# A decoder layer on one core: cached keys and values by pairs, other homes for values, low parts last

## The chip, the cores and the metric

The kernel runs on one core of a Trainium2 chip. The metric is device time in microseconds (us): the kernel before took 955.71 us, the median of three runs (954.79 to 956.05). The engines are named as in the profile: PE is TensorE with its matmuls, PEld its weight loads, DVE is VectorE, ACT is ScalarE, POOL is GpSimd, SP is SyncE, which here only issues DMAs. A name with a q (SPq, ACTq) is an engine's queue in the act of issuing.

## What is computed

One layer of a hybrid decoder for a prompt of 512 rows and for 8 samples of 4 rows each, with the same weights, all in float32. Cut to what matters:

```python
z = rms_norm(x, g_mix_pre) @ w_in                 # 1024 -> mLSTM heads and attention heads
h_ml = mlstm_chunkwise(q, k, v, i_pre, logf, ...) # 4 heads of 128
s = einsum('bqhcd,bkhcd->bhcqk', dq, dk) * 64**-0.5     # differential attention:
p = softmax(where(mask, s, -inf))                       # two components c per head
a = p[:, :, 0] - lam * p[:, :, 1]
h_da = rms_norm(einsum('bhqk,bkhd->bqhd', a, dv), g_da_head) * (1 - lam_init)
x = x + rms_norm(concat([h_ml, h_da]) @ w_out, g_mix_post)
x = x + rms_norm(mem_attend(rms_norm(x, g_mem_pre), mk, mv, w_mq, w_mo), g_mem_post)
f, conv_new = conv_ffn(rms_norm(x, g_ffn_pre), conv_buf, w_up, w_dw, b_dw, w_down)
x = x + rms_norm(f, g_ffn_post)
```

In the attention the samples also read 256 cached positions each, whose pages of 128 lie scattered (cache_dk and cache_dv through page_table). In the cross-attention (mem_attend, 4 heads of 256) the prompt reads 256 memory rows, whose keys and values are computed from mem_prompt (w_mk, w_mv), and each sample reads 256 cached ones (cache_mem_k, cache_mem_v). The cached keys and values, too, go through TensorE only once.

## The kernel before

**Precision.** The large products are made from pairs: an operand is split into a high part (fp32r, a cast on ACT, L146 or L221) and a low part (the rest, a subtraction on POOL or DVE, L147 or L223), and a product is hi·hi + hi·lo + lo·hi, three matmuls (L409 to L411, L467, L479). Rows are normalised, turned by four transposes into one PSUM tile (tp, L330), scaled with the gain on the way out (ht, L332) and split into tiles named hT, hqT or fT: such a tile of four feature groups is a "quad", and two quads hold the 1024 features. In the numbered names, fT00 and fT01 are the high parts of quad 0 and 1, fT10 and fT11 the low parts. The 544 rows are blocks 0 to 3 of 128 prompt rows and block 4 with the 32 sample rows.

**Buffers.** Weights are loaded by SP into the staging pool (tiles wst, six buffers, L231) and split into slots (wslot, pool wp, four buffers with the tag W). `W.nslots` says how many slots may be filled ahead, and `W.pump()` fills them. A second pool, sp, has eleven general buffers (tag S). Two PSUM pools hold five tiles (mm) and three (at).

**What sets the order.** The program is written as coroutines that are stepped against each other, and a scheduler then orders the instructions of every engine; each engine runs its list strictly in that order. `tc.issue_after(x)` holds what stands in its block until x, and `burst(x)` (L343) is the same with high priority, so that a run of matmuls stays together.

**The start.** The memory rows are normalised and turned into memT; the ht tiles behind them are kept, and four DMAs of ACT write them to DRAM (mem_d, L598), held until the second result of the memory keys (mkv, L544). That result is turned (mkt, L548) and copied by ACT (mkT, L550).

**Differential attention.** The prompt's softmax runs as a pipeline of 16 steps: scores (sda, L1229), exponents on ACT (pda, L1233), transposes (tpa, L1245), their copy by ACT (aT, L1247), values (oda, L1255). The samples' cached keys are gathered by SP (L1087), turned into kT tiles (wp buffers, L1209, L1210) and multiplied by the samples' queries, which fill 32 columns (ssc, L1215, four matmuls for each sample). Their values are gathered into staging buffers and summed into ops (L1297, eight matmuls for each sample); a last four (L1305) add the samples' own rows. Two weight slots are reserved in this stage (`W.nslots = 2`), for w_out, whose staging loads stand behind the value gathers on SP.

**Cross-attention.** The samples' memory values come in four tiles of the wp pool (samples 3 to 6) and, for the other samples, in two staging buffers each. They are used in the order 2, 1, 0, 7, 6, 5, 4, 3, and the load of sample 7 is issued last, behind the products of 2, 1 and 0 (pso, L1464), whose staging buffers it takes.

**The way into the FFN.** proj_add makes the projection w_mo by blocks 4, 0, 1, 2, 3, adds it to the residual (xb, L1152), and appends the block to a list of those still to be turned (norm_turn). Here the rows are turned unscaled; their factors (rsd, L1164) are spread over the partitions by a matmul each (rsb, L1584), copied (L1585) and multiplied onto the FFN's first product (L1611). The last two blocks are turned inside the FFN's first four column tiles (gemmB with half_first), which take rows 0 to 255 first (128x256) and rows 256 to 543 after (128x288).

Of the kernel before, what the change touches and what calls it, by code (L numbers as in the profile page):

```python
# [1 line left out]

# [5 lines left out]
F32 = mybir.dt.float32  # L8
# [69 lines left out]
def kernel(ctx: ExitStack, tc: tile.TileContext, I, O):  # L78
# [241 lines left out]

    turned = [None]

    def norm_turn(h, n, gname, xt, c0, pool=(True, False)):

        tmps = []
        for q in range(2):
            ps = at("tp")
            pv = v2(ps, P)[:, :, :n]
            for j in range(4):
                turned[0] = tr(pv[:, j, :], h[:, (4 * q + j) * P:(4 * q + j + 1) * P], ident[:n, :n])  # L330
            tmp = T2([P, 4, n], "ht")
            VTT(out=tmp, in0=pv, in1=gcol(gname, 4 * q, 4 * q + 4).unsqueeze(2).broadcast_to([P, 4, n]), op=MUL)  # L332
# [64 lines left out]
    def gemmA(xt, nk, blocks, evac, block_major=False, before=None, mid=None, halves=False, midk=4):  # L397
# [29 lines left out]
        else:  # L427
# [27 lines left out]
                yield 4 * 0.53  # L455
            yield 0

    def gemmB(xt, evacs, half_first=False):

        if half_first:  # L460
            slots = [W.get() for _ in evacs]
            for i, (c0, c1) in enumerate(HALF):
                for s, ev in zip(slots, evacs):
                    ps = mmp()[:, :c1 - c0]
                    for k in range(8):
                        for j, (l, x) in enumerate(((0, xt.hi), (0, xt.lo), (1, xt.hi))):
                            mm(ps, lhsT=s[:, l, k, :], rhs=x(k, c0, c1), start=(k == 0 and j == 0), stop=(k == 7 and j == 2))  # L467
# [69 lines left out]
    evm = []  # L537

    def mem_k():
        dst = O["p_mem_k"][0, 0].rearrange("t h d -> t (h d)")  # L540
        for i in range(2):
            def ev(b, ps):
                t = Z("mkv")
                evm.append(nc.scalar.mul(out=t, in_=ps, mul=mrs[:, b:b + 1]))  # L544
                nc.scalar.dma_start(out=dst[b * P:(b + 1) * P, 512 * i:512 * i + 512], in_=t)
                pt = at("mkt")
                for j in range(4):
                    tr(pt[:, j * P:(j + 1) * P], t[:, j * P:(j + 1) * P], ident)  # L548
                u = Z("mkT")
                nc.scalar.copy(out=u, in_=pt)  # L550
                nc.scalar.dma_start(out=mk_d[:, 4 * i:4 * i + 4, b * P:(b + 1) * P], in_=v2(u, P))
            yield from gemmA(memT, 8, [0, 1], ev)
# [35 lines left out]
    for i, _ in enumerate(mem_k()):  # L588
        if i in HSTEPS:
            j = HSTEPS.index(i)  # L590
            norm_T(xbs[HB[j]], rows(HB[j])[1], "g_mix_pre", hT, rows(HB[j])[0])
            if j + 2 < 5:
                h_in(HB[j + 2])

    with tc.issue_after(evm[1].ins):
        for b in range(2):
            for q, t in enumerate(kept[b]):
                nc.scalar.dma_start(out=mem_d[:, 4 * q:4 * q + 4, b * P:b * P + P], in_=t)  # L598


    masks = T2([P, MASK_W], "masks")
# [510 lines left out]
    def proj_add(xt, gname, src, gname2, dst, order=None, scale=None):  # L1112

        g = gbc(gname)
        y0, s0, xb, pend, ready, target = {}, {}, {}, [], [], []

        def ssq(b, y, nm):
            n = rows(b)[1]
# [20 lines left out]
        def ev1(b, ps):  # L1139
# [6 lines left out]
            VTT(out=z, in0=ps, in1=g[:n, 512:], op=MUL)  # L1146
            STT(out=ss, in0=s0[b], scalar=EPS, in1=ss, op0=ADD, op1=ADD)
            rs = rstd(ss, n, 1, None)
            x = xb[b]
            for i, z in enumerate((y0[b], z)):  # L1150
                c = slice(512 * i, 512 * i + 512)
# [13 lines left out]
            scale[1].append((rs[:n], c0, n))  # L1165

        def mid():
            if len(pend) > LP:
                norm_turn(*pend.pop(0))

        def second(xt2):
            target.append(xt2)
            run(gemmA(xt, 8, [4, 0, 1, 2, 3], ev1, block_major=True, before=before, mid=mid, midk=1 if scale else MIDK))
            while ready:
# [35 lines left out]
            (VCP if g else nc.scalar.copy)(out=kt[:, :, g * P:(g + 1) * P], in_=v2(ps, P))  # L1210

    def dk_scores(b):
        ps = mmp("ssc")[:, :260]
        for h in range(H):
            mm(ps[NS * h:NS * h + NS], lhsT=qz[:, h, b // 4].rearrange("p c r -> p (c r)"), rhs=kts[b][:, h, :],  # L1215
               start=True, stop=True)
        VTT(out=ps[:, 256:260], in0=ps[:, 256:260], in1=con("cm4"), op=ADD)
        sample_exp(sall, b, ps, nm, su)

    def da_soft(i):  # L1220
        b, h = i // H, i % H
# [65 lines left out]
    vts = {}  # L1287

    def dv_load(b):
        st = vts[b] = stage()  # L1290
        for g in range(2):
            gather("cache_dv", b, g, st[:, 512 * g:512 * g + 512])

    def dv_out(b):
        for g in range(2):
            for h in range(H):
                mm(ops[NS * h:NS * h + NS, :P], lhsT=az[g][:, h, b * NS:(b + 1) * NS],  # L1297
                   rhs=vts[b][:, g * 512 + h * P:g * 512 + (h + 1) * P], start=(b == 0 and g == 0), stop=False)
# [5 lines left out]
    for h in range(H):  # L1304
        mm(ops[NS * h:NS * h + NS, :P], lhsT=anew[:, h].rearrange("p b t -> p (b t)"), rhs=dvS[:, h * P:(h + 1) * P],  # L1305
           start=False, stop=True)
    oS = T2([P, P], "daoS")
    nc.scalar.copy(out=oS, in_=ops[:, :P])
    sq = T2([P, P], "dasq")
# [135 lines left out]

    def mv_load(b):

        if 2 < b < 7:
            t = wp.tile([P, 2, DM], F32, name="vt", tag="W")
            vts[b] = [t[:, 0], t[:, 1]]  # L1450
        else:
            vts[b] = [stage(), stage()]
        for c in range(2):
            dma(out=vts[b][c], in_=I["cache_mem_v"][0, b, c * P:(c + 1) * P].rearrange("t h d -> t (h d)"))
# [123 lines left out]
    rss = []  # L1578

    def spread(i):  # L1580
        while rss and (i or len(rss) > 2):
            rs, c0, n = rss.pop(0)
            ps = at("rsb")
            mm(ps[:, :n], lhsT=rs.broadcast_to([n, P]), rhs=ident[:n, :n], start=True, stop=True)  # L1584
            VCP(out=rsb[:, c0:c0 + n], in_=ps[:, :n])  # L1585
# [63 lines left out]
    def ups_of(gi):  # L1649
# [248 lines left out]
```

## Time and profile before

| | |
|---|---|
| Runs without the profiler, median of 3 | 955.71 us (954.79 to 956.05) |
| The profiled execution's own time | 956.55 us |
| Its span, first to last instruction | 954.8 us |
| Mean granted TensorE clock | 0.997 |
| Instructions | 17089 |
| DMA traffic | 130.27 MB, mean 136 GB/s |

The 40 slices of the span show how evenly TensorE is loaded. Each digit is the busy share of some 24 us in tenths (9 is 90% or more); the last two rows are the DMA engines' share and the traffic:

```profile
PE   8999999999999999999999999999999999999995
DVE  6745144565886438634654769727758676686767
ACT  6545233344676447624544523332212222222232
POOL 7411000025431217300000444001110110111114
DMA  8950023344825439855954743063052312512023
```

A reader looks for the slices below 9 in the first row: only the first and the last. In between the idle time stays under a tenth of every slice and shows only in finer views. In the rows of the timeline that follow further down, the columns are start, length, engine, line, operation, written tile and read tiles, shapes and count; in brackets stands the engine's idle time before, with what ended it. A matmul whose operands stay plain float32 has two records there: the four ssc matmuls of a sample count as x8.

### The profile page before, as it was taken

How to read it: one execution, taken by the hardware profiler on the slowest of the kernel's cores; microseconds unless marked ns; L12 is line 12 of the kernel's file. 1: busy time of each engine (PE TensorE's matmuls, PEld its weight loads, DVE VectorE, ACT ScalarE, POOL GpSimd, SP SyncE). 2: the span in 40 equal slices, each digit the busy share in tenths (PEclk: the TensorE clock that was granted, in tenths of full speed). 3: DMA queues.
4: the chain of work that ended last, by engine and by line, in shares of the span. 5: the costliest groups of instructions: out<-in, count | busy, mean ns of one | idle time of the engine just before them, and what ended most of it. 6: DMA issues, size and time to landing. Idle time of an engine off the chain costs nothing. (4 is left out here: it accounts for less than half of the span.)

```text
span 954.8 us, 17089 instructions
## 1 busy us (share of the span) xinstructions
PE 931.0 (98%) x6612; PEld 808.5 (85%) x6612; DVE 601.9 (63%) x1130; ACT 387.8 (41%) x750; POOL 196.3 (21%) x384
## 2 busy tenths in 40 slices
PE   8999999999999999999999999999999999999995
PEld 5799787889766778998777799989988997999974
DVE  6745144565886438634654769727758676686767
ACT  6545233344676447624544523332212222222232
POOL 7411000025431217300000444001110110111114
PEclk9999999999999999999999999999999999999998
DMA  8950023344825439855954743063052312512023
GB/s 300 280 171 21 1 89 136 89 124 135 269 86 182 147 102 325 299 166 166 355 215 116 205 133 89 4 177 89 4 144 79 122 26 79 164 48 89 24 92 115
DMA packets 120673, 130.27 MB, mean 136 GB/s; under 512 B 8567, under 2 KB 86232, under 8 KB 120592
## 3 DMA queue, kind: packets, MB, share of 16 engines
q1 hardware_dynamic: 114408, 125.69, 41.5%
q10 hardware_dynamic: 6184, 3.48, 1.2%
q8 instruction: 52, 0.85, 0.4%
q14 instruction: 29, 0.24, 0.1%
HBM read 112.22 MB, written 16.93 MB: 135 GB/s over the span
## 5 line engine op out<-in xcount | busy, mean ns | idle before, releaser
L479 PE MATMUL mm<-fT,wslot 128*128 128x256 f32 x1872 | 236.0, 288 | 0.0
L479 PEld LDWEIGHTS mm<-fT,wslot 128*128 128x128 f32 x1872 | 234.4, 188 | 1.8 <-issue 0.8
L146 ACT CAST wslot<-wst 128x1024 fp32r<-128x1024 f32 x125 | 130.8, 1050 | 257.2 <-PE mm L479 72.4
L147 DVE TENSOR_TENSOR wslot<-wst,wslot 128x1024 fp32r<-128x1024 f32 x125 | 154.2, 1237 | 89.0 <-ACT wslot L146 88.6
L1709 PE MATMUL mm<-wslot,act 128*128 128x512 f32 (+1 forms) x180 | 70.2, 391 | 0.0
L1710 PE MATMUL mm<-wslot,act 128*128 128x512 f32 (+1 forms) x180 | 70.0, 392 | 0.0
L1708 PE MATMUL mm<-wslot,act 128*128 128x512 f32 (+1 forms) x180 | 69.3, 387 | 0.0
L1616 POOL COPY cvo<-u 128x2 f32<-128x2 f32 x43 | 12.1, 281 | 204.3 <-DVE u L1614 194.3
L409 PE MATMUL mm<-wslot,hT 128*128 128x512 f32 x128 | 51.2, 402 | 0.0
L411 PE MATMUL mm<-wslot,hT 128*128 128x512 f32 x128 | 51.0, 400 | 0.0
L479 PE MATMUL mm<-hT,wslot 128*128 128x256 f32 (+1 forms) x384 | 50.9, 289 | 0.0
L410 PE MATMUL mm<-wslot,hT 128*128 128x512 f32 x128 | 50.8, 397 | 0.0
L1611 DVE TENSOR_TENSOR u<-mm,rsb 128x256 f32<-128x256 f32 x43 | 18.2, 425 | 51.2 <-PE mm L479 50.3
L479 PEld LDWEIGHTS mm<-hT,wslot 128*128 128x128 f32 x384 | 49.2, 188 | 0.6 <-issue 0.2
L1708 PEld LDWEIGHTS mm<-wslot,act 128*128 128x128 f32 x180 | 34.3, 191 | 8.0 <-issue 0.8
L1710 PEld LDWEIGHTS mm<-wslot,act 128*128 128x128 f32 x180 | 33.8, 188 | 7.3 <-issue 0.4
L1709 PEld LDWEIGHTS mm<-wslot,act 128*128 128x128 f32 x180 | 33.8, 188 | 7.2
L1628 ACT ACTIVATE c<-c 128x560 f32<-128x560 f32 x21 | 14.1, 671 | 56.7 <-DVE c L1622 56.7
L1622 DVE SCALAR_TENSOR_TENSOR c<-u,cvT,c 128x560 f32<-128x560 f32 x43 | 34.3, 798 | 0.9
L1621 DVE SCALAR_TENSOR_TENSOR c<-u,cvT,c 128x560 f32<-128x560 f32 x43 | 34.1, 793 | 0.2
L1721 DVE TENSOR_TENSOR yp<-mm,yp 128x512 f32<-128x512 f32 (+1 forms) x41 | 27.2, 674 | 5.2 <-PE mm L1710 5.1
L411 PEld LDWEIGHTS mm<-wslot,hT 128*128 128x128 f32 x128 | 24.1, 188 | 5.0
(475 smaller groups left out, 1857.2 us busy)
## 6 DMA issues: line engine op xcount, KB each, us to landing
wst<-in_w_up_dram SPq DMA_DIRECT2D x42, 512.0 KB
wst<-in_w_in_dram SPq DMA_DIRECT2D x28, 512.0 KB
wst<-in_w_down_dram SPq DMA_DIRECT2D x20, 512.0 KB
wst<-in_cache_mem_k_dram SPq DMA_DIRECT2D x16, 512.0 KB
wst<-in_w_mk_dram SPq DMA_DIRECT2D x8, 512.0 KB
xb<-in_x_prompt_dram SPq DMA_DIRECT2D x8, 512.0 KB
wst<-in_cache_dk_dram SPq DMA_DIRECT2D x16, 256.0 KB
wst<-in_cache_dv_dram SPq DMA_DIRECT2D x16, 256.0 KB
```

The source lines that it names most:

```text
L146: nc.scalar.copy(out=hi, in_=src)
L147: (eng or nc.vector).tensor_tensor(out=lo, in0=src, in1=f32(hi), op=SUB)
L409: mm(ps[b], lhsT=xt.hi(k, c0, c0 + n), rhs=s[:, 0, kk, :], start=(k == 0), stop=False)
L410: mm(ps[b], lhsT=xt.hi(k, c0, c0 + n), rhs=s[:, 1, kk, :], start=False, stop=False)
L411: return mm(ps[b], lhsT=xt.lo(k, c0, c0 + n), rhs=s[:, 0, kk, :], start=False, stop=(k == nk - 1))
L479: mm(ps[i], lhsT=s[:, l, k, :], rhs=x(k, c0, c1), start=(k == 0 and j == 0), stop=(k == 7 and j == 2))
L1621: STT(out=c, in0=u[:, 1:EXT - 1], scalar=w[1], in1=c, op0=MUL, op1=ADD)
L1622: STT(out=c, in0=u[:, 0:EXT - 2], scalar=w[0], in1=c, op0=MUL, op1=ADD)
L1708: mm(ps, lhsT=t[:, 0, c0:c0 + P], rhs=s[:, 0, i % 2, cs], start=st, stop=False)
L1709: mm(ps, lhsT=t[:, 0, c0:c0 + P], rhs=s[:, 1, i % 2, cs], start=False, stop=False)
L1710: return mm(ps, lhsT=t[:, 1, c0:c0 + P], rhs=s[:, 0, i % 2, cs], start=False, stop=en)
L1721: VTT(out=y, in0=ps, in1=y, op=ADD)
```

## The change

- **Start.** The four writes of the memory rows are emitted right behind the loop over the row blocks, without a hold.
- **gemmB with half_first** goes through a tile's 24 matmuls in another order: for quad 0 the high rows against both parts of the weights, the same for quad 1, then the low rows of both quads.
- **proj_add** keeps the residual addition in a list (`late`) where the rows are turned unscaled, and makes it in the middle of the next block; that of block 2 is held until the second scaling (ht) of the turn before. Each waiting block is turned there, where one was kept back so far.
- **Cached keys** (dk_scores) and **values** (dv_out) are taken by two samples in one run of matmuls; the samples' own rows (L1305) join the last run.
- **Values** are gathered into wp tiles, two samples each, and no slot is reserved for weights in this stage (`W.nslots = 0`).
- **Memory values** of sample 7 get a tile of the general pool and are loaded with those of samples 3 to 6.
- **The factors** (spread) go through one PSUM tile for each half of the rows: three copies, five before.
- **The last two turns** inside the FFN's first tiles are held until the matmul that was emitted last.

The core of the diff:

```diff
@@ gemmB
-                    for k in range(8):
-                        for j, (l, x) in enumerate(((0, xt.hi), (0, xt.lo), (1, xt.hi))):
-                            mm(ps, lhsT=s[:, l, k, :], rhs=x(k, c0, c1), start=(k == 0 and j == 0), stop=(k == 7 and j == 2))
+                    for k0, l, x in ((0, 0, xt.hi), (0, 1, xt.hi), (4, 0, xt.hi), (4, 1, xt.hi), (0, 0, xt.lo), (4, 0, xt.lo)):
+                        for k in range(k0, k0 + 4):
+                            done[0] = mm(ps, lhsT=s[:, l, k, :], rhs=x(k, c0, c1), start=(k == 0 and l == 0 and x == xt.hi),
+                                         stop=(k == 7 and x == xt.lo))
@@ start
-    with tc.issue_after(evm[1].ins):
-        for b in range(2):
-            for q, t in enumerate(kept[b]):
-                nc.scalar.dma_start(out=mem_d[:, 4 * q:4 * q + 4, b * P:b * P + P], in_=t)
+    for b in range(2):
+        for q, t in enumerate(kept[b]):
+            nc.scalar.dma_start(out=mem_d[:, 4 * q:4 * q + 4, b * P:b * P + P], in_=t)
@@ proj_add
+            late.append((b, z, rs))
+            if not scale:
+                add(*late.pop(0))
+        def add(b, z, rs):
...
-            if len(pend) > LP:
+            if len(pend) > (0 if scale else LP):
                 norm_turn(*pend.pop(0))
+            if late:
+                with tc.issue_after(scaled[0].ins) if late[0][0] == 2 else nullcontext():
+                    add(*late.pop(0))
@@ dk_scores
+        if b % 2 == 0:
+            return
...
+        for c in (b, b - 1):
+            pair[c] = mmp("ssc")[:, :260]
+            for h in range(H):
+                with burst(t):
+                    t = mm(pair[c][NS * h:NS * h + NS], lhsT=qz[:, h, c // 4].rearrange("p c r -> p (c r)"), rhs=kts[c][:, h, :],
+                           start=True, stop=True).ins
@@ differential attention
-    W.nslots = 2
+    W.nslots = 0
@@ dv_load
-        st = vts[b] = stage()
+        if b % 2 == 0:
+            t = wp.tile([P, 2, 1024], F32, name="vt", tag="W")
+            vts[b], vts[b + 1] = t[:, 0], t[:, 1]
@@ dv_out
+        for c, g in ((b, 1), (b, 0), (b - 1, 0), (b - 1, 1)):
             for h in range(H):
+                with burst(t):
...
@@ mv_load
-        if 2 < b < 7:
-            t = wp.tile([P, 2, DM], F32, name="vt", tag="W")
+        if 2 < b:
+            t = wp.tile([P, 2, DM], F32, name="vt", tag="W") if b < 7 else S([P, 2, DM], F32, "vt")
...
-    for b in range(3, 7):
+    for b in range(3, NB):
         mv_load(b)
...
-    mv_load(7)
@@ ups_of
-                    norm_turn(*pend.pop(0))
+                    with tc.issue_after(done[0].ins):
+                        norm_turn(*pend.pop(0))
```

How this moves instructions is shown at three places. First ScalarE's list at the start, before and after; memT are the memory rows' casts, hN the squares of a norm, mem_d the writes in question (L600 after the change):

```order
L146 CAST memT_138<-ht 128x4x128 x2
L309 ACTIVATE hN,ssq<-xm 128x1024
L221 CAST wslot<-wst 128x1024
L146 CAST memT_138<-ht 128x4x128 x2
L221 CAST wslot<-wst 128x1024 x3
L309 ACTIVATE hN,ssq<-xb 128x1024 x2
```

```order
L146 CAST memT_138<-ht 128x4x128
L600 DMA mem_d<-ht 128x4x128
L146 CAST memT_138<-ht 128x4x128
L309 ACTIVATE hN,ssq<-xm 128x1024
L600 DMA mem_d<-ht 128x4x128
L146 CAST memT_138<-ht 128x4x128
L221 CAST wslot<-wst 128x1024
L600 DMA mem_d<-ht 128x4x128
L146 CAST memT_138<-ht 128x4x128
L600 DMA mem_d<-ht 128x4x128
L221 CAST wslot<-wst 128x1024 x3
```

The four writes now stand among the first casts, and one cast of the second memory block has come ahead of a weight cast.

Next ScalarE's list in the differential attention, where the first w_out slots are cast (wslot), again before and after. The exponents (pda), the output's scaling (dao) and the copy aT belong to the prompt's softmax; their lines are L1233, L1257 and L1247 before and L1255, L1279 and L1269 after:

```order
L1233 ACTIVATE pda,su<-sda,nm 128x512 x2
L146 CAST wslot<-wst 128x1024
L1257 ACTIVATE dao<-oda,rc 128x128
L1247 COPY aT<-tpa 128x384
L146 CAST wslot<-wst 128x1024 x2
L1233 ACTIVATE pda,su<-sda,nm 128x512 x2
```

```order
L146 CAST mixT_3109<-dtm 128x4x128
L146 CAST wslot<-wst 128x1024
L1279 ACTIVATE dao<-oda,rc 128x128
L1269 COPY aT<-tpa 128x384
L1255 ACTIVATE pda,su<-sda,nm 128x512 x2
L146 CAST wslot<-wst 128x1024
L1279 ACTIVATE dao<-oda,rc 128x128
L1269 COPY aT<-tpa 128x384
L146 CAST wslot<-wst 128x1024
L1255 ACTIVATE pda,su<-sda,nm 128x512
```

The first cast has moved ahead of the first exponents over 512 columns, and no two casts stand next to each other.

Last TensorE's list at the FFN's start, with the numbers of the buffers; the four wslot tiles are the first four column tiles:

```order
L1584 MATMUL rsb_6324<-cpk_87,rsd_6027 128x32
L1584 MATMUL rsb_6327<-cpk_87,rsd_6071 128x128
L467 MATMUL mm_6299<-fT00_6090,wslot_5939 128x256
L467 MATMUL mm_6355<-fT00_6090,wslot_5944 128x256
L467 MATMUL mm_6384<-fT00_6090,wslot_6235 128x256
L467 MATMUL mm_6431<-fT00_6090,wslot_6246 128x256
L467 MATMUL mm_6299<-fT10_6091,wslot_5939 128x256
L467 MATMUL mm_6299<-fT00_6090,wslot_5939 128x256 x2
```

```order
L1619 MATMUL rsb_6319<-cpk_87,rsd_6026 128x32
L1619 MATMUL rsb_6319<-cpk_87,rsd_6094 128x128
L1619 MATMUL rsb_6319<-cpk_87,rsd_6156 128x128
L472 MATMUL mm_6294<-fT00_6074,wslot_5934 128x256 x8
L472 MATMUL mm_6347<-fT00_6074,wslot_5939 128x256 x8
L472 MATMUL mm_6376<-fT00_6074,wslot_6230 128x256 x8
L472 MATMUL mm_6423<-fT00_6074,wslot_6241 128x256 x6
L472 MATMUL mm_6294<-fT01_6086,wslot_5934 128x256 x8
L472 MATMUL mm_6294<-fT10_6075,wslot_5934 128x256 x4
L472 MATMUL mm_6294<-fT11_6087,wslot_5934 128x256 x4
L332 MATMUL tp_6329<-cpk_87,xb_5986 128x128 x4
```

The low parts (fT10, fT11) have moved from the fifth matmul to the 39th, the third factor (rsb) ahead of all of them, and block 2 is turned behind 46 matmuls.

More of the change, by code (lines that the diff above doesn't have):

```diff
@@ L1 @@
[L1 removed]
+from contextlib import nullcontext, ExitStack, contextmanager
 import concourse.bass as bass
@@ L1114, in proj_add @@
         g = gbc(gname)
-        y0, s0, xb, pend, ready, target = {}, {}, {}, [], [], []
+        y0, s0, xb, pend, ready, target, late = {}, {}, {}, [], [], [], []
         def ssq(b, y, nm):
@@ L1173, in second @@
             run(gemmA(xt, 8, [4, 0, 1, 2, 3], ev1, block_major=True, before=before, mid=mid, midk=1 if scale else MIDK))
+            while late:
+                add(*late.pop(0))
             while ready:
@@ L1212, in dk_scores @@
     def dk_scores(b):
[L1213 to L1218, printed above, removed]
+        if b % 2 == 0:
+            return
+        pair = {}
+        t = None
+        for c in (b, b - 1):
[4 more added lines that the diff above has]
+                           start=True, stop=True).ins
+        for c, ps in pair.items():
+            VTT(out=ps[:, 256:260], in0=ps[:, 256:260], in1=con("cm4"), op=ADD)
+            sample_exp(sall, c, ps, nm, su)
     def da_soft(i):
@@ L1289, in dv_load @@
     def dv_load(b):
-        st = vts[b] = stage()
+        if b % 2 == 0:
+            t = wp.tile([P, 2, 1024], F32, name="vt", tag="W")
+            vts[b], vts[b + 1] = t[:, 0], t[:, 1]
         for g in range(2):
-            gather("cache_dv", b, g, st[:, 512 * g:512 * g + 512])
+            gather("cache_dv", b, g, vts[b][:, 512 * g:512 * g + 512])
     def dv_out(b):
-        for g in range(2):
+        if b % 2 == 0:
+            return
+        t = None
+        for c, g in ((b, 1), (b, 0), (b - 1, 0), (b - 1, 1)):
             for h in range(H):
-                mm(ops[NS * h:NS * h + NS, :P], lhsT=az[g][:, h, b * NS:(b + 1) * NS],
-                   rhs=vts[b][:, g * 512 + h * P:g * 512 + (h + 1) * P], start=(b == 0 and g == 0), stop=False)
+                with burst(t):
+                    t = mm(ops[NS * h:NS * h + NS, :P], lhsT=az[g][:, h, c * NS:(c + 1) * NS],
+                           rhs=vts[c][:, g * 512 + h * P:g * 512 + (h + 1) * P], start=(c == 1 and g == 1), stop=False).ins
+        if b == NB - 1:
+            for h in range(H):
+                with burst(t):
+                    t = mm(ops[NS * h:NS * h + NS, :P], lhsT=anew[:, h].rearrange("p b t -> p (b t)"), rhs=dvS[:, h * P:(h + 1) * P],
+                           start=False, stop=True).ins
     for t, _ in enumerate(pipe(NB, dv_load, lambda b: None, dv_out)):
@@ L1580, in spread @@
     def spread(i):
-        while rss and (i or len(rss) > 2):
+        if len(rss) <= (0 if i else 2):
+            return
+        ps = at("rsb")
+        for _ in range(len(rss) - (0 if i else 2)):
             rs, c0, n = rss.pop(0)
-            ps = at("rsb")
-            mm(ps[:, :n], lhsT=rs.broadcast_to([n, P]), rhs=ident[:n, :n], start=True, stop=True)
-            VCP(out=rsb[:, c0:c0 + n], in_=ps[:, :n])
+            c = c0 - HALF[i][0] if c0 < SEQ else 256
+            mm(ps[:, c:c + n], lhsT=rs.broadcast_to([n, P]), rhs=ident[:n, :n], start=True, stop=True)
+        VCP(out=rsb[:, HALF[i][0]:HALF[i][0] + 256], in_=ps[:, :256])
+        if i == 0:
+            VCP(out=rsb[:, SEQ:], in_=ps[:, 256:256 + NS])
     proj, second = proj_add(oT, "g_mem_post", lambda b: xd[0][rows(b)[0]:rows(b)[0] + rows(b)[1], :], "g_ffn_pre", xd[1],
```

12 lines of the change are left out of this document (5 added, 7 removed).

## The prediction

> **What bounds the kernel now.** I read the shares of busy time first, then TensorE's waits grouped by what ended them, then stretches of 20 us, and only then the rows of the places that the change touches.
>
> ```profile
> span 954.8 us, 17089 instructions
> PE 931.0 (98%) x6612; PEld 808.5 (85%) x6612; DVE 601.9 (63%) x1130; ACT 387.8 (41%) x750; POOL 196.3 (21%) x384
> ```
>
> TensorE (PE) is busy for 931.0 of 954.8 us. The change can win only where TensorE is idle, 954.8 − 931.0 = 23.8 us, or by making its work itself shorter. In the stretches the columns are the window, its length and the busy time of PE, its weight loads, VectorE (DVE), ScalarE (ACT) and GpSimd (POOL), then clock, DMA share and GB/s.
>
> ```profile
> 0.00:20.00 20.00, 17.17 (x70) 10.97 (x71) 13.76 (x16) 13.75 (x21) 14.56 (x22) 1.00 0.89 300
> 280.00:300.00 20.00, 17.82 (x218) 11.46 (x210) 12.60 (x25) 12.20 (x35) 3.81 (x4) 1.00 0.56 184
> 480.00:500.00 20.00, 18.63 (x151) 13.81 (x150) 12.06 (x29) 9.21 (x19) 0.00 (x0) 1.00 0.58 208
> 540.00:560.00 20.00, 18.72 (x139) 17.28 (x138) 18.61 (x28) 11.56 (x21) 13.05 (x20) 1.00 0.70 227
> 600.00:620.00 20.00, 20.00 (x128) 18.31 (x127) 15.68 (x26) 5.65 (x8) 1.69 (x10) 1.00 0.02 5
> 940.00:960.00 20.00, 3.65 (x28) 3.31 (x26) 9.75 (x15) 3.59 (x10) 6.08 (x7) 0.80 0.25 92
> ```
>
> The clock is full, so nothing is to be had there. The last stretch holds 14.8 − 3.65 = 11.2 us of the idle time, behind the last matmuls, where the change alters nothing; a stretch like 600 to 620 us holds none. What is left, some 12 us, lies at the start, in the differential attention (245 to 302 us), at 481 us and at the start of the FFN (545 to 562 us), and these are the places that the change touches. The waits, as line, cause, us in total, times and longest:
>
> ```profile
> PE mm L467 <- POOL fT L147: 1.8, 2, 1.3
> PE tp L330 <- ACT mkT L550: 1.5, 1, 1.5
> PE pso L1464 <- DMA wst<-in_cache_mem_v_dram: 1.4, 1, 1.4
> PE oda L1255 <- ACT aT L1247: 1.1, 2, 0.9
> PE tpa L1245 <- DVE pda L1237: 0.7, 1, 0.7
> PE spt L1078 <- ACT spc L1075: 0.7, 1, 0.7
> PE tpa L1245 <- ACT pda L1233: 0.6, 1, 0.6
> PE sda L1229 <- ACT pda L1233: 0.6, 1, 0.6
> PE mkt L548 <- ACT mkv L544: 0.4, 1, 0.4
> ```
>
> The reader is to see that every wait is short and stands once or twice: the change is a list of small repairs, and its worth is a sum of single waits.
>
> **1. Cached keys and values by pairs.** A cached sample's four matmuls use 32 output columns, and stand among matmuls of full width.
>
> ```profile
> 250.08 0.65 PE L1215 MATMUL ssc<-kT,qz 128*32 128x260 f32 x8 [0.32 <-DVE kT L1210]
> 250.65 1.27 PE L1209 MATMUL tpk<-cpk,wst 128*128 128x128 f32 x8
> 464.92 1.07 PE L1073 MATMUL spa<-cas,csz 128*32 128x256 f32 x16
> 465.92 1.19 PE L1415 MATMUL cpo<-pT,mvN 128*128 128x512 f32 x4
> ```
>
> A run of 8 records lasts from 250.08 to the next instruction at 250.65, 0.57 us, one of 16 records of the same width 1.00 us (464.92 to 465.92). With a fixed part f and a part p for 8 records, f + p = 0.57 and f + 2p = 1.00, so f = 0.14 us for each run. By the order, keys and values make 13 such runs before and 8 after, with the same matmuls in them: 5 × 0.14 = **−0.7 us**. The ends are 0 (if f is the neighbours' pipeline, which stays) and −0.7; I take −0.7, since both pairs of rows are of this shape. Of the 0.32 us wait ahead of the first run I count nothing: a pair now waits for its second sample's keys, too.
>
> **2. Values in tiles of the weights' size, no slots reserved, w_out early.** Before, SyncE's queue (SP) sends the 16 value gathers into the staging buffers and w_out's six loads behind them:
>
> ```profile
> 256.83 30.64 SPq L1087 DMA_DIRECT2D wst<-in_cache_dv_dram  x16
> 287.58 11.82 SPq L231 DMA_DIRECT2D wst<-in_w_out_dram  x6
> 294.37 1.04 ACT L146 CAST wslot<-wst 128x1024 fp32r<-128x1024 f32 x1 [2.72 <-DMA wst<-in_w_out_dram]
> 296.11 0.94 PE L1255 MATMUL oda<-dvN,aT 128*128 128x128 f32 x6 [0.90 <-ACT aT L1247]
> L1215 PE MATMUL ssc<-kT,qz x64: 382/395/407, 250.1 to 274.9; 128*32 128x260 f32 x64
> L1297 PE MATMUL ops<-wst,daz x128: 272/273/298, 284.6 to 298.7; 128*32 128x128 f32 x128
> ```
>
> ScalarE stands at the w_out cast for 2.72 us with the softmax's copies (aT) and exponents (pda) queued behind it, and TensorE waits for these: 1.1 for aT, of it 0.90 here, and 0.6 for pda at L1229, 1.7 us together. After, the values have places of their own, five of the w_out loads go out ahead of the value gathers, and the casts stand singly between softmax operations. A cast of 1.04 us still holds a softmax operation now and then, so I take three quarters, **−1.3 us**; the ends are −1.7 and, if single casts hold back as much, 0. What can be late next is the values, which now take the places of used-up keys. The last two rows (a line's matmuls, with first and last start) show keys in use from 250.1 to 274.9 and values from 284.6 to 298.7, in the same order of samples: a pair's values are wanted some 24 to 34 us behind its keys, and its four gathers took 4 × 30.64 / 16 = 7.7 us, even while they waited for staging buffers. I count no wait. The other waits here (0.7 spt, 0.7 and 0.6 tpa) belong to softmax steps that stay, but move among each other: 0 as my value, −2.0 to +0.7 (one more of them) as the ends.
>
> **3. The last sample's memory values.** The wait of 1.4 us at L1464 is a load into staging buffers that came free too late:
>
> ```profile
> 451.13 6.32 SPq L1454 DMA_DIRECT2D wst<-in_cache_mem_v_dram  x6
> 475.56 0.81 SPq L1454 DMA_DIRECT2D wst<-in_cache_mem_v_dram  x2
> 481.60 1.07 PE L1464 MATMUL pso<-wst,caz 128*32 128x256 f32 x16 [1.37 <-DMA wst<-in_cache_mem_v_dram]
> ```
>
> The two loads went out at 475.56, 6 us before use. After, they fill a tile of the general pool and stand in SP's order ahead of the six of 451.13, some 30 us before use, and no wait for those six is in the list: **−1.4 us**; at the other end it is 0, if that tile comes free as late.
>
> **4. Start of the FFN.** The first matmuls need the normalised rows as a high part, which ScalarE makes, and a low part, which GpSimd subtracts behind it.
>
> ```profile
> 545.61 0.74 PE L467 MATMUL mm<-fT,wslot 128*128 128x256 f32 x4
> 547.63 3.11 PE L467 MATMUL mm<-fT,wslot 128*128 128x256 f32 x24 [1.28 <-POOL fT L147]
> 550.58 0.38 PE L1584 MATMUL rsb<-cpk,rsd 128*128 128x128 f32 x2
> 537.93 1.41 DVE L1152 SCALAR_TENSOR_TENSOR xb<-y,rs,xb 128x512 f32<-128x512 f32 x2 [0.86 <-POOL rs L304]
> 544.78 3.35 DVE L1152 SCALAR_TENSOR_TENSOR xb<-y,rs,xb 128x512 f32<-128x512 f32 x2
> 544.63 2.95 POOL L147 TENSOR_TENSOR fT<-ht,fT 128x512 fp32r<-128x512 f32 x2
> ```
>
> Before, the fifth matmul is the first that needs a low part, 0.7 us after the start. After, 30 matmuls with the high parts of the first four of the eight feature groups (quad 0) come first, 8 of the other four (quad 1) next, and the first low part at the 39th: 24 matmuls take about 2.95 us (547.63 to 550.58), 0.12 each, so it is needed 38 × 0.12 = 4.6 us after the start. Three subtractions of 2.95 / 2 = 1.5 us are ahead of it at most, so the wait of 1.28 goes. VectorE also scales the two row halves of block 1 ahead of the residual additions of block 2, so quad 1 is there. The other wait of this group, 1.8 − 1.3 = 0.5, stands at the second half of the rows, and I keep it: blocks 2 and 3 are now turned after 46 and 78 matmuls, earlier than their additions may be ready. So **−1.3 us**, with −1.8 and 0 as the ends, and +1.9 in the rival below. The scales' copies, five before and three now, lie on VectorE beside matmuls and count nothing; the same reordered loop for the first projection and the queries shows no wait before and counts nothing either, unless the start's inputs come later.
>
> **5. The memory tiles written out at once.** Four DMA issues of ScalarE stood behind the first result:
>
> ```profile
> 40.85 0.95 ACTq L598 DMA_DIRECT2D mem_d<-ht  x2
> 43.59 1.23 ACTq L598 DMA_DIRECT2D mem_d<-ht  x1
> 44.86 1.44 ACTq L598 DMA_DIRECT2D mem_d<-ht  x1
> 47.49 0.43 PE L330 MATMUL tp<-cpk,hN 32*128 32x32 f32 x4 [1.51 <-ACT mkT L550]
> ```
>
> The last two hold ScalarE for 2.67 us, behind them stands the copy mkT, and behind that TensorE's 1.51 us; 0.44 (mkt, L548) belongs to the same knot. Both go: −1.95. The four issues now lie between the first casts. There, an issue among free queues costs ScalarE 0.95 / 2 = 0.5 us each, 1.9 in all, of which about half reaches TensorE, since the memory rows' casts also come ahead of a weight cast: +1.0. **−0.9 us**; the ends are −1.95 and, with four issues at 1.44 and the traffic not hidden, a loss (rival D).
>
> **Sum:** −0.7 − 1.3 − 1.4 − 1.3 − 0.9 = −5.6 us. The profiled execution took 956.55 us (1.75 more than its span), so it would be 950.95. The median of the runs shown is 955.71, 0.84 lower; there the same sum gives **950.1 us**.
>
> **The rivals.** A: the waits come back elsewhere. In an order that every engine follows strictly, an earlier TensorE meets the next late operand; only the shorter runs and the value load of part 3, which have no successor that I can name, remain: −2.1, 953.6 us. For it speaks that VectorE is busy for 18.61 of 20 us at 540; against it that the stretches behind each place are full.
>
> B: all waits of the touched places go, with the regrouped softmax also the three of 0.7, 0.7 and 0.6: −0.7 − 1.7 − 1.4 − 1.8 − 1.95 − 2.0 = −9.55, 946.2 us.
>
> C: VectorE becomes the bound at the FFN's start. Two residual additions take 1.41 us at 537.93, but 3.35 at 544.78, over the very time in which GpSimd subtracts (544.63 to 547.58). After, three GpSimd subtractions stand in a row beside such additions; if these and the scaling behind them are late by 3.35 − 1.41 = 1.9 us on the path of blocks 2 and 3, part 4 is +1.9 instead of −1.3: −2.4, 953.3 us. The Trainium skill, "SBUF — State Buffer", section "SBUF: two separate sides", has a rule of that kind: a VectorE operation with two SBUF inputs and a GpSimd operation that reads SBUF exclude each other for a whole instruction. The 3.35 us agree with it; by the rule alone the sum would be that of rival C, while without it part 4 keeps its −1.3.
>
> D, the slower side: the write-out at the start delays the weights. The DMA share there is 0.89 at 300 GB/s. The four tiles are 1 MB, 3.5 us at that rate, and with four issues of 1.44 (5.8 us) on ScalarE between the weight casts, up to 9.3 us are added in place of +1.0: −5.6 + 8.3 = +2.7, 958.4 us. It decides once TensorE uses up its lead over the casts; the waits of the start in the list are no longer than 0.4 to 1.5 us, which speaks against the whole price. That the change does not do what it says is excluded by the order: the instructions do stand elsewhere.
>
> **How the numbers follow.** The forecast has 0.52, A 0.15, B 0.10, C 0.13, D 0.10. A measurement can tell about 0.2% from no change, 1.9 us: below 953.8 is faster, above 957.6 slower. Faster: 0.50 of the forecast, half of A, all of B, 0.08 of C, about 0.75. Same: the rest of these, 0.15. Slower: D, 0.10. The range reaches from B to a us past A, 946.2 to 954.6; D and some 0.08 of the rests stay outside.
>
> **What would show it.** Right: no wait of pso for the memory values, none of aT or pda behind a w_out cast, no fT wait near 547 us, the run of ssc at 16 records and about 1.0 us, no tp wait for mkT. Wrong: new waits of ops for the values, of half the FFN's rows for fT above 0.5 us, or less busy TensorE in the first 40 us. It would be wrong above all if the first 40 us lose more than a us, or if the attention's softmax, not the w_out cast, sets the pace there.

## The result, and the profile after

The changed kernel took 950.34 us (median of 6 runs, 948.88 to 952.3) against 955.88 us (6 runs, 954.79 to 957.41): the ratio is 0.9942, with a 95% interval from 0.9926 to 0.9958. In a later round it was 950.22 us (6 runs) against 957.63 (11 runs), 0.9933 with 0.9916 to 0.9949. The forecast of 950.1 us lay 0.2 us from the first median, but of its five terms one was too large and another too small by about as much.

From the page of the changed kernel, and from the list of its waits of TensorE (line, cause, us in total, times, longest):

```profile
span 948.7 us, 17078 instructions
PE 927.8 (98%) x6612; PEld 807.9 (85%) x6612; DVE 599.7 (63%) x1128; ACT 387.5 (41%) x750; POOL 198.9 (21%) x384
```

```profile
PE tpa L1267 <- DVE pda L1259: 1.4, 2, 1.1
PE tp L332 <- DMA xm<-in_mem_prompt_dram: 1.3, 1, 1.3
PE mm L413 <- POOL memT L147: 1.2, 2, 1.0
PE mm L411 <- ACT memT L146: 1.2, 1, 1.2
PE oda L1277 <- ACT aT L1269: 0.9, 2, 0.6
PE tpk L1223 <- ACT kT L1224: 0.5, 1, 0.5
PE mm L472 <- ACT fT L146: 0.3, 1, 0.3
```

The waits of pso (1.4 us), of fT on GpSimd (1.8) and of tp for mkT (1.5) are gone. Others are new or longer: at the start the memory rows' load (xm, 1.3) and memT (2.4, where the kernel before had 1.0), in the attention tpa for VectorE's pda (1.4, before 0.7) and the keys' turn tpk. The span is 6.1 us shorter, but TensorE's idle time fell only from 23.8 to 20.9 us; the other 3.2 us (931.0 to 927.8) stand in the profile as busy time of the same 6612 records. So the list of waits is no ledger. A ledger needs landmarks: matmuls that stand in the same place in both programs. The rows give first and last start of four groups, before and after:

```profile
L673 PE MATMUL mm<-hT,wgs x16: 276/288/299, 67.3 to 71.0; 128*128 128x256 f32 x8, 128*128 128x288 f32 x8
L479 PE MATMUL mm<-hqT,wslot x192: 276/288/366, 409.2 to 438.3; 128*128 128x256 f32 x96, 128*128 128x288 f32 x96
L1415 PE MATMUL cpo<-pT,mvN x48: 387/394/500, 462.5 to 498.8; 128*128 128x512 f32 x48
L1708 PE MATMUL mm<-wslot,act x180: 278/389/499, 610.8 to 943.1; 128*128 128x512 f32 x172, 128*128 128x256 f32 x8
```

```profile
L675 PE MATMUL mm<-hT,wgs x16: 280/289/299, 66.5 to 70.3; 128*128 128x256 f32 x8, 128*128 128x288 f32 x8
L485 PE MATMUL mm<-hqT,wslot x192: 276/288/366, 406.6 to 435.7; 128*128 128x256 f32 x96, 128*128 128x288 f32 x96
L1447 PE MATMUL cpo<-pT,mvN x48: 388/394/496, 459.9 to 494.8; 128*128 128x512 f32 x48
L1747 PE MATMUL mm<-wslot,act x180: 278/389/499, 604.6 to 937.0; 128*128 128x512 f32 x172, 128*128 128x256 f32 x8
```

Between the start, the first gate matmul, the first query matmul of this line (L479, L485), the last cpo and the first act matmul lie four stretches, and behind them the rest. The line takes the second half of the queries' columns; the first half (L467, L472) starts 25 us earlier and lies, with all that follows the gates, in the stretch called attention. Worked out so for every profile of this study (us):

| profile | start | attention | cross-attention | FFN start | rest |
|---|---|---|---|---|---|
| before | 67.3 | 341.9 | 89.6 | 112.0 | 344.0 |
| r_before (again) | 67.2 | 341.2 | 89.4 | 112.2 | 344.0 |
| after | 66.5 | 340.1 | 88.2 | 109.8 | 344.1 |
| r_after (again) | 69.1 | 340.5 | 88.1 | 109.8 | 344.0 |
| u_memd | 67.5 | 339.9 | 88.1 | 110.0 | 344.2 |
| u_order | 65.9 | 340.3 | 88.2 | 111.7 | 343.8 |
| u_pairs | 66.2 | 341.1 | 88.1 | 109.7 | 344.6 |
| u_tiles | 64.5 | 341.0 | 88.1 | 110.0 | 344.2 |
| u_mv7 | 64.6 | 340.3 | 89.9 | 109.9 | 344.1 |
| u_late | 64.5 | 340.3 | 88.2 | 110.9 | 344.1 |
| m_memd0 | 70.5 | 339.9 | 88.1 | 110.1 | 343.9 |
| m_wg | 65.5 | 340.1 | 88.2 | 109.8 | 344.5 |
| s_memd | 65.5 | 340.4 | 88.2 | 109.5 | 344.3 |
| x_wg | 65.2 | 340.1 | 88.1 | 109.9 | 344.1 |

Where an edit does not touch a stretch, it repeats within 0.2 us in the cross-attention, 0.7 in the attention, 0.6 at the FFN's start, and 0.8 in the rest. The start alone varies by far more, with one and the same program. Most variants were timed only once (949.55 to 954.34 us), on several chips, and their totals move with the start; so what follows compares stretches, and a difference in the attention of under 0.7 us rests on little.

### The profile page after: what moved, and what is told of

Same layout as the page of the kernel before. It is cut to its first block, busy times and chain, and to the rows that moved or that the text cites. A ratio compares the mean times of both kernels' runs of the same rounds, so it can differ in the third digit from the quotient of the medians.

```text
span 948.7 us, 17078 instructions
## 1 busy us (share of the span) xinstructions
PE 927.8 (98%) x6612; PEld 807.9 (85%) x6612; DVE 599.7 (63%) x1128; ACT 387.5 (41%) x750; POOL 198.9 (21%) x384
## 5 line engine op out<-in xcount | busy, mean ns | idle before, releaser
L485 PE MATMUL mm<-fT,wslot 128*128 128x256 f32 x1872 | 235.9, 288 | 0.0
L485 PEld LDWEIGHTS mm<-fT,wslot 128*128 128x128 f32 x1872 | 234.4, 188 | 1.8 <-issue 0.8
L485 PE MATMUL mm<-hT,wslot 128*128 128x256 f32 (+1 forms) x384 | 51.0, 289 | 0.0
L485 PEld LDWEIGHTS mm<-hT,wslot 128*128 128x128 f32 x384 | 49.2, 188 | 0.5 <-issue 0.2
```

## Experiments: each part taken back

**u_memd**, the writes held again:

```diff
+    with tc.issue_after(evm[1].ins):
+        for b in range(2):
...
```

> The changed kernel with the memory writes held until the second mkv again. Theory M, the moved writes win the start: the first gate matmul (mm<-hT,wgs), at 66.5 us after and 67.3 before, goes back to about 67.3, the wait of tp for mkT (1.5 us) is back, the kernel is 0.8 us longer. Rival O, the new order of the 24 matmuls wins the start, and the moved writes only cost (ScalarE held for 2.75 us): the first gate matmul comes at 66.5 or earlier, down to 65.3.

The first gate matmul came at 67.5, tp waited 1.0 us for mkT and mkt 0.4. Theory M holds for this pair of profiles; what the early writes win varies from profile to profile, as the start does.

**u_order**, the 24 matmuls in the old order:

```diff
-                    for k0, l, x in ((0, 0, xt.hi), (0, 1, xt.hi), (4, 0, xt.hi), (4, 1, xt.hi), (0, 0, xt.lo), (4, 0, xt.lo)):
+                    for k in range(8):
+                        for j, (l, x) in enumerate(((0, xt.hi), (0, xt.lo), (1, xt.hi))):
```

> The changed kernel with the old order of the 24 matmuls (high, low, high for each feature group). By theory M the start stays (first gate matmul at 66.5), by rival O it goes to about 67.3. For the FFN: theory F, low parts last win there: the stretch from the last cpo matmul to the first one of act (109.8 us after, 112.0 before) grows by 1.3 to 1.8, with fT waits on POOL back. Rival L, the residual additions moved behind the turns win it: the stretch grows by 0.5 at most.

The FFN's start grew by 1.9, and the wait for the low part is back (timeline of TensorE, start, length, and in brackets the idle time with its cause):

```profile
543.78 5.23 PE L472 MATMUL mm<-fT,wslot 128*128 128x256 f32 x42 [1.73 <-POOL fT L147]
```

Theory F holds, a little above its bound of 1.8. The start was 65.9 us, within what the new order shows, so rival O falls.

**u_pairs**, one sample at a time:

```diff
-        if b % 2 == 0:
-            return
+        ps = mmp("ssc")[:, :260]
...
```

> The changed kernel with cached keys and values one sample at a time, as before. Theory: five more 32-column runs at 0.14 us each, the stretch from the first gate matmul to the first query matmul (mm<-hqT), 340.1 us after and 341.9 before, grows by 0.7. Rival: softmax waits take up what the runs save (tpa for pda on DVE is 1.4 us after and 0.7 before): it grows by 0.2 at most or shrinks.

The attention grew to 341.1, by 1.0 and 0.6 beside the two profiles of the changed kernel, in spite of shorter waits (between 246 and 322 us TensorE's idle times add up to 3.0 us, in place of 3.6 and 4.0). So the theory's direction holds, and the runs themselves save more than 0.7. Rows of the kernel before show the part that was left out: a step before a run of 32 columns, too, is longer. The last two rows, of the changed kernel, show a run of 16 records.

```profile
283.69 0.22 PE L1230 MATMUL sda<-cb 128*128 128x128 bf16 x1
283.75 0.86 PE L1229 MATMUL sda<-dkT,dqz 128*128 128x384 f32 x2
284.45 0.22 PE L1230 MATMUL sda<-cb 128*128 128x128 bf16 x1
284.60 0.86 PE L1297 MATMUL ops<-wst,daz 128*32 128x128 f32 x22
252.58 1.08 PE L1236 MATMUL ssc<-kT,qz 128*32 128x260 f32 x16
253.59 0.65 PE L1039 MATMUL mlt<-cpk,mlh 128*128 128x128 f32 x4
```

The same matmul (L1230) is followed after 0.06 us by one of full width, and after 0.15 by the run: 0.09 us at the entry beside the 0.14 of the prediction, which the run of 16 bears out: it takes 1.01 us (252.58 to 253.59), two of 8 take 2 × 0.57 = 1.14. Five runs are then 5 × 0.23 = 1.15 us by this estimate. The trace of u_pairs has 14 such runs, six more than the changed kernel's 8: 1.4 us, less the 0.6 and 1.0 of waits that come with the pairs, is 0.8 and 0.4 beside the measured 1.0 and 0.6.

**u_tiles**, values in staging buffers, two slots reserved:

```diff
-            t = wp.tile([P, 2, 1024], F32, name="vt", tag="W")
-            vts[b], vts[b + 1] = t[:, 0], t[:, 1]
+        st = vts[b] = stage()
...
-    W.nslots = 0
+    W.nslots = 2
```

> The changed kernel with the values in staging buffers and two weight slots reserved again (pairs kept). Theory: the w_out casts hold ScalarE again, aT and pda waits of 1.1 to 1.7 us are back, the stretch from the first gate matmul to the first query matmul grows from 340.1 to 341.3 or more. Rival: the old waits came from the single runs' places in the order, and it grows by 0.3 at most.

The attention took 341.0, 0.5 to 0.9 more: between theory and rival, and little above the 0.7 by which this stretch varies. The w_out cast stood for 2.72 us as in the kernel before, but with the pairs kept other instructions were queued behind it:

```profile
292.31 1.05 ACT L146 CAST wslot<-wst 128x1024 fp32r<-128x1024 f32 x1 [2.72 <-DMA wst<-in_w_out_dram]
297.92 0.66 PE L1267 MATMUL tpa<-cpk,pda 128*128 128x128 f32 x4 [0.20 <-DVE pda L1259]
```

TensorE shows only 0.2 us of idle time near it, and its idle times between 246 and 322 us add up to 3.9, within those of the changed kernel (3.6 and 4.0). The cast's wait was thus not worth 1.7 us by itself; what took the 0.5 to 0.9 stays open.

**u_mv7**, the last sample's values as before:

```diff
-        if 2 < b:
+        if 2 < b < 7:
...
+    mv_load(7)
```

> The changed kernel with sample 7's memory values loaded last into staging buffers, as before. Theory: the wait of pso for them is back with 1.4 us, the stretch from the first query matmul to the last cpo matmul grows by 1.4 (88.2 us after, 89.6 before), nothing else changes. Rival: another wait was only moved, it grows by 0.5 at most.

```profile
477.56 1.07 PE L1496 MATMUL pso<-wst,caz 128*32 128x256 f32 x16 [1.65 <-DMA wst<-in_cache_mem_v_dram]
```

The stretch grew from 88.2 to 89.9: a recorded wait of 1.65 cost 1.7 us. Theory.

**u_late**, residual additions and turns where they were:

```diff
-            if not scale:
-                add(*late.pop(0))
+            add(*late.pop(0))
...
-            if len(pend) > (0 if scale else LP):
+            if len(pend) > LP:
```

> The changed kernel with the residual additions and the turns of the unscaled rows where they were (the new order of the 24 matmuls kept). Theory F, the order of the matmuls wins the FFN's start: the stretch from the last cpo matmul to the first of act, 109.8 us after and 111.7 with the old order, grows by 0.4 at most. Rival L2, both are needed, since a late turn takes the cover away: it grows by 1 or more, with a wait for fT or for tp's xb near 547 us.

It grew by 1.1, as rival L2 said, with a wait for the high part of fT: the additions stood ahead of the second scaling again, and took 3.38 us beside GpSimd's subtractions.

```profile
539.30 3.38 DVE L1159 SCALAR_TENSOR_TENSOR xb<-y,rs,xb 128x512 f32<-128x512 f32 x2
543.74 0.68 DVE L334 TENSOR_TENSOR ht<-tp,gT 128x512 f32<-128x512 f32 x1
540.14 4.47 PE L472 MATMUL mm<-fT,wslot 128*128 128x256 f32 x32
545.12 3.66 PE L472 MATMUL mm<-fT,wslot 128*128 128x256 f32 x29 [0.52 <-ACT fT L146]
```

Both parts are needed: low parts last, and the high parts early enough. No run takes back the held turns of the last two blocks or the factors' shared PSUM tiles; their share is not shown.

## Experiments: the start

In the profile after, ScalarE stands ahead of the first write (ACTq is its queue while it issues; the idle time shows at the next cast):

```profile
8.57 0.61 ACT L146 CAST memT<-ht 128x512 fp32r<-128x512 f32 x1
11.49 0.40 ACTq L600 DMA_DIRECT2D mem_d<-ht  x1
11.94 0.62 ACT L146 CAST memT<-ht 128x512 fp32r<-128x512 f32 x1 [2.75 <-DMA wg<-in_w_in_dram]
```

The write reads ht and has nothing to do with wg. But the trace holds the completion semaphore of every DMA: the program uses eight of them again and again, and a DMA is not issued before the one ahead of it on the same semaphore has landed. The first write has the semaphore of wg's load. That load was issued at 1.86 us, in 1024 pieces of 32 bytes, and landed at 11.47; the write went out at 11.49. The Trainium skill, "DMA: Bandwidth & Descriptors", section "Anatomy of one DMA — SWDGE (gpsimd) path", says that a DMA's semaphore wait happens on the issuing sequencer; the section is on DMAs that GpSimd issues, and these rows of ScalarE agree, since the casts behind the write stood still for 2.75 us. Three ways around it were tried.

**m_memd0**, the writes held until the first mkv:

```diff
+    with tc.issue_after(evm[0].ins):
+        for b in range(2):
...
```

> The changed kernel with the memory writes held until the first mkv (about 22 us). Theory W, the early writes lose part of their gain because ScalarE's first write waits for the slow load of wg (0 to 2.75 us in the runs so far, first gate matmul at 64.5 to 66.5): that wait is gone, the first gate matmul comes at 65.4 (67.4 less the 1.95 of mkv and mkT) or earlier. Rival T, traffic and not the wait sets the start: it comes at 66 to 67, since the weights' transfers are then delayed later.

It missed both, at 70.5 us. The fourth write waited again, and ScalarE with it: by its semaphore for a load of w_in, issued at 21.25 us and landed at 32.79. (The cast's row names a landing that came a little later, at 33.02, but the write had gone out by then.)

```profile
32.81 0.37 ACTq L603 DMA_DIRECT2D mem_d<-ht  x1
33.22 0.62 ACT L146 CAST hT<-ht 128x512 fp32r<-128x512 f32 x1 [6.69 <-DMA out_dram<-mkv]
38.91 1.94 PE L332 MATMUL tp<-cpk,hN 128*128 128x128 f32 x8 [3.08 <-DVE hN L318]
```

**m_wg**, wg loaded behind the first mkv:

```diff
-    SQ.dma_start(out=wg, in_=w_in...
+    with tc.issue_after(evm[0].ins):
+        SQ.dma_start(out=wg, in_=w_in...
```

> The changed kernel with the early writes kept, and the load of wg (1024 pieces of 32 bytes, first of its queue) issued behind the first mkv. Theory W: the first write no longer waits for wg's landing, memT is cast at about 9 us, the first gate matmul comes at 64.5 or earlier, 1 to 2 us ahead of 66.5. Rival T: the first gate matmul stays within 65.8 to 66.8.

The first write went out at 7.39 us, but now the fourth one waited for the landing of the first, at 16.14 us. ScalarE stood for 2.91 us at the cast behind it, and the gate matmul came at 65.5, between theory and rival.

```profile
16.16 0.37 ACTq L602 DMA_DIRECT2D mem_d<-ht  x1
16.57 2.11 ACT L221 CAST wslot<-wst 128x1024 fp32r<-128x1024 f32 x2 [2.91 <-DMA mem_d<-ht]
```

**s_memd**, the writes issued by SP:

```diff
-            nc.scalar.dma_start(out=mem_d[:, 4 * q:4 * q + 4, b * P:b * P + P], in_=t)
+            nc.sync.dma_start(out=mem_d[:, 4 * q:4 * q + 4, b * P:b * P + P], in_=t)
```

> The changed kernel with the four memory writes issued by SP, among its loads at about 18 to 20 us. Theory W, what the writes cost is the time for which ScalarE stands at their issue: it stands nowhere now, the first gate matmul comes at 64.5 us or earlier, and the kernel is at or up to 1 us under the changed one. Rival T, it is the traffic: the x rows and w_in behind the writes come 3.5 us later (1 MB at 300 GB/s), TensorE waits for them near 30 to 40 us as in the run that held the writes until the first mkv, and the first gate matmul comes at 67 to 70.

Rival T falls: with the same four writes, issued at 18 to 21 us, the gate matmul came at 65.5, and TensorE shows no wait of more than 0.25 us between 20 and 60 us. Theory W missed by a us. The casts stand as in the kernel before, and its waits for memT (0.6 and 0.4) and mrs (0.5) are back; beside that kernel the start is 1.8 us earlier, near the 1.95 of the two waits that the prediction counted before any price. The time was 950.37 us (5 runs, 949.66 to 950.69), ratio 0.9928 (0.9914 to 0.9943): no better than the changed kernel within the intervals, but without its runs near 953.

**r_after** and **r_before**, both kernels again:

> The changed kernel once more, to see how its start varies. If ScalarE's wait for wg's landing (0 to 2.75 us so far) explains the start, the first gate matmul comes at 64.5 without such a wait and up to 2 us later with it; if not, the two do not go together. All other stretches within 0.3 us of the first profile.

> The kernel before once more. Its start has no early write and so nothing that waits for wg: the first gate matmul comes at 67.3 within 0.3, and the other stretches within 0.3 us of the first profile. Rival: the start varies by 1 us or more here, too, and then it is the loads that vary, not ScalarE's wait.

The changed kernel stood for 3.36 us this time, and its gate matmul came at 69.1: later, as the wait would have it, but by 4.6 us beside 64.5, not the 2 that were expected. Its attention, 0.4 longer, also missed the 0.3. The kernel before repeated its start with 67.2. Its attention was 0.7 shorter than in the first profile, more than expected: pda's wait of 0.6 at L1229 was not there.

**x_wg**, wg's load from contiguous rows:

```diff
-    SQ.dma_start(out=wg, in_=w_in[:, 4 * MLW:4 * MLW + 8].rearrange("(k p) n -> p k n", p=P))
+    SQ.dma_start(out=wg, in_=w_in[:P, 0:64].rearrange("p (k n) -> p k n", k=8))
```

> The changed kernel with the load of wg replaced by one of the same size from contiguous rows (128 pieces of 256 bytes; so the gates are computed from other weights, and the outputs behind them differ). Theory W: the first write no longer waits for a late landing, ScalarE is held for 0.2 us at most, the first gate matmul comes at 64.5 within 0.5, and the times lie together near the lowest of the changed kernel (949 to 950). Rival T: the start goes on varying from 64.5 to 69, since the other loads vary.

No write waited for wg, and the first went out at 7.51 us. But the fourth one waited for a load of w_mk, issued at 7.11 us and landed at 13.82, and so ScalarE was held for 1.23 us, not 0.2. The gate matmul came at 65.2, 0.2 later than theory W allowed.

```profile
13.84 0.37 ACTq L600 DMA_DIRECT2D mem_d<-ht  x1
14.25 2.00 ACT L221 CAST wslot<-wst 128x1024 fp32r<-128x1024 f32 x2 [1.23 <-DMA wst<-in_w_mk_dram]
```

The times were 949.22 to 951.3 us (5 runs, median 949.67); the two near 953.3 of the six in r_after have no counterpart, though these runs are from another chip, and a spread of 2 us is left, which the loads themselves may make. One cast of a weight slot stands one place earlier in this program, so it is not quite the same order.

Put together, ScalarE's stand ahead of a write and the first gate matmul, in the profiles with writes by ScalarE and the new order of matmuls:

| profile | stand, us | at the write | first gate matmul, us |
|---|---|---|---|
| u_mv7 | 0.55 | fourth | 64.6 |
| u_late | 0.75 | first | 64.5 |
| u_tiles | 0.87 | first | 64.5 |
| x_wg | 1.23 | fourth | 65.2 |
| u_pairs | 2.49 | first | 66.2 |
| after | 2.75 | first | 66.5 |
| m_wg | 2.91 | fourth | 65.5 |
| r_after | 3.36 | first | 69.1 |
| m_memd0 | 6.69 | fourth | 70.5 |

A stand of under a us is covered; beyond that a longer one goes with a later start, if not in proportion. The table does not separate the stand from slow loads: where wg landed late, the first weight load often did, too. The first weight cast starts at 7.1 to 7.2 us in u_late, u_tiles and u_mv7, at 7.6 in u_pairs and after, at 8.5 in r_after. The two profiles of the kernel before differ there as well (6.57 and 7.24), yet not in the start.

The writes also hold SyncE, which the prediction did not count. Loads of gain vectors reuse the writes' semaphores and wait for their landing (16.72 us for the first write), and the three loads of w_mk behind them go out at 18.2 us in place of 14.3 (before, then after):

```profile
14.30 3.05 SPq L231 DMA_DIRECT2D wst<-in_w_mk_dram  x3
18.22 1.45 SPq L231 DMA_DIRECT2D wst<-in_w_mk_dram  x3
```

What that costs by itself was not run.

## Why the prediction was right, step by step

- **The sum.** −0.7 − 1.3 − 1.4 − 1.3 − 0.9 = −5.6 was forecast, and the first two profiles differ by −0.8 (start) − 1.8 (attention) − 1.4 − 2.2 + 0.1 = −6.1; the medians differ by −5.5. That TensorE's single waits are what counts was right for the memory values and the FFN's start, and the rest behind them stayed as it was. In the attention and at the start waits went and others came, so that the sum came so near owes something to luck.
- **1 and 2, the attention:** −2.0 forecast, −1.8 in the first pair of profiles; the ten profiles with neither part undone, and the two of before, lie at about 340.2 and 341.6, which is −1.4. Two sizes were off. The price of a run was 0.23, not 0.14, since only its end had been looked at. And the term of −1.3 for w_out was too large: undone, it costs 0.5 to 0.9 in the one profile of u_tiles. The waits for aT and pda in the one profile were taken as the property of the cast, but the second profile of the same kernel lacks one of them, and under the pairs the same stand of 2.72 us cost TensorE little. The waits behind the w_out casts did go (after, TensorE has none above 0.15 us between 284 and 300), but others came: between 246 and 322 us the idle times add up to 4.1 and 3.2 us in the two profiles of before, to 3.6 and 4.0 in the two of after. So the shorter runs, 1.15 by the estimate above, are likely most of the −1.4.
- **3, the memory values:** −1.4 forecast, −1.4 measured, 1.7 when undone. Right in mechanism and size.
- **4, the FFN's start:** −1.3 forecast, −2.2. The mechanism held (low parts last, with the high parts early enough), the term was mis-sized. The second wait of 0.5, which I kept, shrank to 0.3. And a recorded wait is less than what TensorE loses: before, four matmuls start at 545.61 and the fifth at 547.63, so with 0.12 each 547.63 − 545.61 − 0.48 = 1.54 us were lost where the row says 1.28, because the profile gives the four records 0.74 us. That is 1.54 + 0.2 of the 2.2; the rest is not shown.
- **5, the start:** −0.9 forecast, −0.8 in the profile, but by other sums, and the agreement is luck. The seven profiles with ScalarE's writes at once and wg unchanged start at 64.5 to 69.1, 65.9 on average, the three with late writes (before, r_before, u_memd) at 67.2 to 67.5: −1.4 on average, between −2.8 and +1.8. mkT and mkv were won as forecast; the writes' issues took 0.40 to 0.87 us each, 0.58 on average where 0.5 was estimated, but a stand of 0.6 to 3.4 us came on top, which the working did not have. It named traffic and issue time as the risk, not a landing that an issue waits for.
- **Rivals.** C: the addition beside GpSimd was slow again, 2.88 us for two against 1.40 a little later, but with 46 matmuls of cover it held nothing up:

```profile
543.55 2.88 DVE L1160 SCALAR_TENSOR_TENSOR xb<-y,rs,xb 128x512 f32<-128x512 f32 x2
550.72 1.40 DVE L1160 SCALAR_TENSOR_TENSOR xb<-y,rs,xb 128x512 f32<-128x512 f32 x2
541.69 5.71 PE L472 MATMUL mm<-fT,wslot 128*128 128x256 f32 x46
547.25 1.04 PE L332 MATMUL tp<-cpk,xb 128*128 128x128 f32 x8
```

  So the slowing weighed there is in the rows and decides nothing here. A came about in small, in the attention and at the start; B did not. D came about in part: ScalarE was held, by a landing, and the start lost 1.8 us against the kernel before in r_after and 3.2 in m_memd0. As a price for traffic alone it does not stand: u_late and u_tiles, whose writes go out from 9 to 13 us, have the earliest start, 64.5.

## What to carry to other kernels

Price a change to a nearly full engine by its single waits, measured from start to start, and check it by landmarks of stretches, not by the list of waits. A DMA issue on a computing engine is not only its issue time: look for what its semaphore waits for, and put such issues where nothing is queued behind them. Before a wait in one profile becomes a term, look whether a second profile of the same kernel has it.

## What the runs showed of the hardware

- A run of matmuls with 32 columns among full ones costs about 0.23 us: 0.09 at its entry (0.15 in place of 0.06) and 0.14 at its end (two runs of 8 records 1.14, one of 16 1.01). This is an estimate from rows of the cached keys and values.
- A load of 32 KB in 32-byte pieces, issued at 1.86 us among 512 KB loads, landed at 11.5 us; in the other profiles that issue it then, between 8.3 and 12.9.
- The program's DMAs share eight completion semaphores; a write of ScalarE was held until an unrelated load on the same one had landed (11.47 and 11.49 us), and the casts behind it for 2.75 us.
- Two VectorE additions of 128x512 took 1.4 us alone, and 2.9 to 3.4 beside GpSimd's subtractions.
